# A two-layer encoder on one core: the second layer's attention stage with every engine's instructions in program order

## The chip, the cores and the metric

The kernel runs on one core of a Trainium2 chip. The core has five engines with queues of their own: TensorE (PE; its weight loads are listed as PEld), VectorE (DVE), ScalarE (ACT), GpSimd (POOL) and SyncE (SP), from which nearly all DMA transfers are issued. The metric is the device time of one execution in microseconds. For the kernel before it is 1228.63 us, the median of three runs (1226.69 to 1229.92).

## The reference

The reference is a trunk of two pre-norm attention layers on 1024 tokens of width 1024, in float32, with a final RMSNorm. Only the second layer matters here:

```
def odd_layer(x, mem_n, table, norm_g, w_in, ...):
    h = rmsnorm(x, norm_g)
    q1, q2, k1, k2, v, xq, gate = _split(h @ w_in, ODD_SPLITS)
    ...
    # 6 heads, in blocks of 128 queries:
    s = einsum("ibqhd,ibshd->ibhqs", qi, kk) * (D ** -0.5)
    p = softmax(s + rel_bias, axis=-1)
    w = p[0] - lam * p[1]
    y_c = einsum("bhqs,bshe->bqhe", w, v)
    ...
    y_c = rmsnorm(y_c, subln_g) * (1.0 - lam_init)
    y_x = memory_cross_attention(xq, mem_n, w_mem_kv)    # 4 heads, 256 memory tokens
    y = concatenate([y_c, y_x]) * silu(gate)
    return x + y @ w_out
```

Each of the six heads has two score maps; their softmaxes are subtracted with a factor lam, and the result weighs v.

## The kernel before

The kernel is written with a framework in which the program text issues instructions on named engines and takes tiles from pools with a tag and a number of buffers. At compile time the framework simulates the engines with a model of durations, and draws up each engine's queue from it: of the instructions that are ready, the one that the text has first. So an instruction that waits in the model can be passed by a later one of the same engine, and a load can move far ahead of its place in the text. On the chip each queue then runs as drawn up. `tc.issue_after(ins)` adds an order to single instructions; the text uses it in a few places (L1511 to L1515, and where finish() is called).

The second layer's attention is one call of run_steps over 56 steps: 8 cross-attention steps of 128 queries, then 6 heads with 8 blocks of 128 queries. Iteration i of its loop traces, in this order:

1. hooks(i). For i above 9 this is early.step(), up to 32 times, so for i = 10 to 41. It stores the piece of the output weight that the iteration before made (two DMAs, wo10h/wo10l or wo11h/wo11l), loads the next piece (wor, 128 KB), copies it on ACT (L270) and subtracts on POOL (L271): a split into a high and a low part. For i = 3 it loads the first bias tile.
2. hop of step i - 1: a DMA that copies the finished weights e into er, the form in which they are transposed.
3. s1 of step i: TensorE makes the two score maps (sc, eight matmuls, L1505 and L1514) into both PSUM buffers with the tag S; for each map DVE adds the bias and takes the minimum (L1520) and ACT exponentiates (L1523). In the second block of a head the next head's bias tile is loaded (toep, with two copies on POOL). At a head's first block the projections of its k and q are finished ahead of s1.
4. Two pulls of the projection jobs, eight matmuls each (acc, L329). A job is one 128-column tile of the layer's input projection, 48 matmuls in two halves of 512 tokens, so with three pulls an iteration each half takes an iteration. Where a job starts, the next job's weights are loaded (wr, two DMAs of 256 KB), cast on DVE (wh, L241) and subtracted on POOL (wl, L243). At the end of a half its consumer is traced: for k a cast on ACT (L1419), a subtraction on DVE (L1420) and four row DMAs (ck); for q a cast on ACT (L350), a subtraction on DVE (L351) and four row DMAs (cq), high and low parts in turn; for v a copy on ACT and four transposes (tv) later on; for a gate two instructions. The jobs of a head come as v, gate, then the next head's k and q.
5. Posts, one of each pair in turn. d1, in odd iterations: TensorE's ssqc, two activations on ACT (L1567) and a power on POOL (L231). d2, in even ones: TensorE's rbcc, DVE's L1578 and POOL's product with the gate (L1581); with a head's last pair the store of y.
6. s3, in even iterations, for the pair that ended with step i - 3: 16 matmuls (oc), ACT's copy (L1550), DVE's add (L1551), ACT's square (L1553), DVE's L1556.
7. s2 of step i - 2: eight transposes in two halves of four (te, L580), each half with a cast on ACT (L347) and a subtraction on DVE (L348) into PT.
8. finish of step i: DVE's L1528, L1530 and L1532 make the weighted difference of the two maps in e.
9. One pull of eight matmuls, or none more when the projections are over: then the pulls, two an iteration, run the first part of the output projection (pre, L702), for which y is loaded back in chunks (yr).

Buffers that bear on the order: the tag wr has two buffers, shared by wor, the job weights and the chunks of y; the PSUM tag T has two, shared by ssqc, rbcc, te and tv; the PSUM tag S has two, both taken by one step.

Of the kernel before, what the change touches and what calls it, by code (L numbers as in the profile page):

```python
# [3 lines left out]

# [1 line left out]

# [82 lines left out]
class Jobs:  # L89
# [59 lines left out]
    def drain(self):  # L149
        self.step = 10 ** 9  # L150
        while self._advance():
            pass


@with_exitstack
def encoder_kernel(ctx, tc, A):
# [76 lines left out]
    def load_w(src, after=None, fast=False):  # L233
        his, los = [], []
        for kh in range(2):
            raw = wp.tile([P, 4, P], F32, tag="wr", name="wr", bufs=2)
            dma(raw, src[:, 4 * kh:4 * kh + 4, :])
            hi = wp.tile([P, 4, P], F32R, tag="wh", name="wh", bufs=4)
            lo = wp.tile([P, 4, P], F32R, tag="wl", name="wl", bufs=4)
            with (tc.issue_after(after[0]) if after else nullcontext()):  # L240
                nc.vector.tensor_copy(hi, raw)  # L241
            with (tc.issue_after(after[1]) if after else nullcontext()):
                (nc.vector if fast else nc.gpsimd).tensor_tensor(out=lo, in0=raw, in1=hi, op=ALU.subtract)  # L243
            his.append(hi)
            los.append(lo)
        return his, los
# [228 lines left out]
    def run_steps(steps, jobs, hooks=None, pace=None):  # L475
        n = len(steps)
        posts = deque()
        p2 = p3 = 0
        finish = None
        for i in range(n + LAG + 1):  # L480
            behind = None
            if jobs is not None:
                jobs.step = i
            if hooks:
                hooks(i)
            if 0 < i <= n and steps[i - 1].hop:
                steps[i - 1].hop()
            if i < n:
                if steps[i].need:
                    jobs.ensure(*steps[i].need)  # L490
                finish = steps[i].s1()
            f = steps[min(i, n - 1)].fill
            if jobs is not None:
                if half[0] and len(wout) >= 8 and jobs.projected():
                    f = pace(i)
                two = f > 1 and p3 < n and p3 + steps[p3].lag + 1 <= i and steps[p3].s3b is not None
                jobs.pull(f - f // 2 - two)
                if hooks:
                    hooks(-1)
            for q in list(posts):  # L500
                q.pop(0)()
                if not q:
                    posts.remove(q)
            if p3 < n and p3 + steps[p3].lag + 1 <= i:
                st, p3 = steps[p3], p3 + 1
                if st.s3 is not None:
                    if st.need3:
                        jobs.ensure(*st.need3)
                    r = st.s3()
                    if r:  # L510
                        posts.append(r)
                    if st.s3b is not None:
                        jobs.pull(two)
                        st.s3b()
            if p2 < n and p2 + steps[p2].lag <= i:
                behind = steps[p2].s2()
                p2 += 1
            if finish:
                with (tc.issue_after(behind.ins) if behind is not None else nullcontext()):
                    finish()  # L520
                finish = None
            if jobs is not None:
                jobs.pull(f // 2)
                if hooks:
                    hooks(-1)
        while posts:
            for q in list(posts):
                q.pop(0)()
                if not q:
                    posts.remove(q)  # L530
# [276 lines left out]
    last = [None]  # L807
# [185 lines left out]
    jobs = Jobs(jl, ld)  # L993
# [73 lines left out]
    steps = x_steps(M, X, gates, 3, lambda h, qb: (Xq[h], qb * P), 0)  # L1067
# [393 lines left out]
    jobs = Jobs(jl, lambda j: load_w(j["src"], fast=j["tag"] in FAST or j["tag"] == "g7"))  # L1461
# [16 lines left out]
    steps = x_steps(M, X, gates, 3, lambda h, qb: (Xq1[(h, qb // 4)], (qb % 4) * P), 1)  # L1478
# [115 lines left out]
        if i < 0:  # L1594
            wout_hook(1, jobs, "g5", r2)

    run_steps(steps, jobs, hooks1, lambda i: 2)
    jobs.drain()
    left.close()
    st1 = ExitStack()  # L1600
    out_proj(1, None, st1)
# [72 lines left out]
```

## Time and profile before

| | |
|---|---|
| median of 3 runs | 1228.63 us (1226.69 to 1229.92) |
| the profiled execution's span | 1228.9 us |
| TensorE busy | 1196.5 us (97%) |
| DVE busy | 801.1 us (65%) |
| ACT busy | 663.1 us (54%) |
| POOL busy | 436.3 us (36%) |
| the stage of the change | about 628 to 1161 us of the span |
| mean granted TensorE clock | 0.996 |

The profile is of one execution. A row of a timeline has the start and the duration of an instruction (or of a run of like ones, x their number), its engine, its line, its operation, the tiles it writes and reads, and in brackets how long the engine was idle ahead of it and what ended that. "SPq" rows are DMA issues on SyncE; L175 is the helper through which all of them go. The rows of DMA issues grouped by tile end with the KB of each and the median time from issue to landing. Busy TensorE is modelled and overlaps from one matmul to the next: the spacing of their starts says more than their durations.

### The profile page before, as it was taken

The page shows a single profiled execution, that of the slowest core. Times are in us where ns is not written, and L with a number is a line of the kernel's source. Part 1 is how long each engine was busy: PE and PEld are TensorE (multiplying, and loading weights), DVE is VectorE, ACT ScalarE, POOL GpSimd, SP SyncE. Part 2 cuts the span into 40 slices and gives each one's busy share as a digit, 9 for nine tenths or more (in the row PEclk, how much of TensorE's full clock was granted, in tenths as well). Part 3 has the DMA queues.
Part 4 walks back from the last instruction along what each step waited for, and adds up shares of the span by engine and source line. Part 5 has one row for each costly group of instructions (what it writes and reads, how often), then busy time and mean ns, then how long its engine had stood idle before and what let it go on. Part 6 is the DMA issues. An engine that isn't in the chain of part 4 may idle for free.

```text
span 1228.9 us, 19560 instructions
## 1 busy us (share of the span) xinstructions
PE 1196.5 (97%) x6614; PEld 988.4 (80%) x6614; DVE 801.1 (65%) x1495; ACT 663.1 (54%) x1477; POOL 436.3 (36%) x414
## 2 busy tenths in 40 slices
PE   6999999999999999999999999999999999999997
PEld 5788888888888777888888777777787777777886
DVE  5547665377778878635365866766767767667544
ACT  6248754366667766636157744555545454445332
POOL 5023365366665455437112222333143231301100
PEclk9999999999999999999999999999999999999999
DMA  6664445545465565457645445355363452468354
GB/s 257 200 194 147 163 172 163 166 160 207 163 233 209 208 227 191 151 196 237 186 158 156 153 146 164 121 183 163 124 187 125 153 171 105 149 212 285 121 192 155
DMA packets 114304, 216.70 MB, mean 176 GB/s; under 512 B 13302, under 2 KB 47478, under 8 KB 114204
## 3 DMA queue, kind: packets, MB, share of 16 engines
q1 hardware_dynamic: 114060, 215.25, 52.5%
q8 instruction: 53, 0.87, 0.3%
q14 instruction: 47, 0.39, 0.1%
q10 hardware_dynamic: 144, 0.20, 0.0%
HBM read 87.71 MB, written 39.86 MB: 104 GB/s over the span
## 4 chain that ended last, share of the span: by engine, by line
PE 47%; DVE 2%; DMA 1%; issue 1%; ACT 1%; POOL 0%; POOLq 0%; SPq 0%; DVEq 0%; ACTq 0%
PE acc L329 24%; PE po L702 5%; PE oc L1545 3%; PE sc L1505 3%; PE te L580 3%; PE sc L1514 2%; PE pre L702 2%; PE oc L1547 2%; DMA wr<-in_w_in 1%; PE ssqc L1563 1%; PE ox L656 0%; PE rbcc L1576 0%; PE tv L439 0%; PE sx L543 0%; DVE e L1520 0%
## 5 line engine op out<-in xcount | busy, mean ns | idle before, releaser
L329 PE MATMUL acc<-h,wh 128*128 128x512 f32 x1536 | 499.5, 398 | 1.6 <-DVE h L351 0.8
L329 PEld LDWEIGHTS acc<-h,wh 128*128 128x128 f32 x1536 | 282.4, 188 | 65.7 <-issue 7.9
L329 PE MATMUL acc<-h,wl 128*128 128x512 f32 x768 | 303.8, 396 | 1.5 <-POOL wl L243 1.2
L243 POOL TENSOR_TENSOR wl<-wr,wh 128x512 fp32r<-128x512 f32 x94 | 124.8, 1329 | 286.3 <-DVE wh L241 155.0
L1523 ACT ACTIVATE e<-e,mn 128x1024 f32<-128x1024 f32 x96 | 110.0, 1148 | 117.0 <-DVE mn L1520 116.9
L329 PEld LDWEIGHTS acc<-h,wl 128*128 128x128 f32 x768 | 144.3, 188 | 34.9 <-issue 4.4
L1114 POOL TENSOR_TENSOR e<-e,rz 128x1024 f32<-128x1024 f32 x48 | 91.6, 1910 | 84.2 <-DVE rz L1113 57.8
L1520 DVE CUSTOM_DVE_ANT_0 e<-sc,toep 128x1024 f32<-128x1024 f32 x96 | 113.5, 1218 | 8.0 <-PE sc L1514 7.3
L580 PEld LDWEIGHTS te<-identr,er 128*128 128x128 f32 x896 | 92.2, 143 | 18.8 <-PE sa L543 2.2
L580 PE MATMUL te<-identr,er 128*128 128x128 f32 x896 | 99.9, 246 | 4.3 <-DVE O L1578 1.4
L348 DVE TENSOR_TENSOR PT<-te,PT 128x512 fp32r<-128x512 f32 x112 | 74.3, 687 | 42.8 <-ACT PT L347 39.2
L241 DVE CAST wh<-wr 128x512 fp32r<-128x512 f32 x112 | 58.2, 522 | 42.9 <-PE acc L329 17.3
L348 DVE TENSOR_TENSOR PTl<-te,PTh 128x512 fp32r<-128x512 f32 x112 | 74.0, 684 | 9.4 <-ACT PTh L347 8.9
L1545 PE MATMUL oc<-PT,v 128*128 128x512 f32 x192 | 69.8, 403 | 0.7 <-DVE ckl L1420 0.7
L1532 DVE SCALAR_TENSOR_TENSOR e<-e,mr 128x1024 f32<-128x1024 f32 x48 | 66.3, 1381 | 1.5
L347 ACT CAST PT<-te 128x512 fp32r<-128x512 f32 x112 | 62.7, 589 | 7.2 <-PE te L580 6.7
L347 ACT CAST PTh<-te 128x512 fp32r<-128x512 f32 x112 | 62.2, 586 | 7.9 <-PE te L580 7.1
L702 PE MATMUL po<-woh,yh 128*128 128x512 f32 (+1 forms) x172 | 65.7, 382 | 0.0
L702 PE MATMUL po<-woh,yl 128*128 128x512 f32 (+1 forms) x172 | 65.5, 381 | 0.0
L702 PE MATMUL po<-wol,yh 128*128 128x512 f32 (+1 forms) x172 | 65.3, 380 | 0.0
L1105 DVE TENSOR_REDUCE mn<-sb 128x1 f32<-128x1024 f32 x48 | 58.3, 1216 | 7.0 <-PE sb L543 6.6
L350 ACT ACTIVATE yh<-yr 128x256 fp32r<-128x256 f32 (+2 forms) x56 | 24.0, 447 | 66.2 <-DMA yr<-ysc 37.5
(211 smaller groups left out, 2358.7 us busy)
## 6 DMA issues: line engine op xcount, KB each, us to landing
er<-e SPq DMA_DIRECT2D x112, 512.0 KB, 3.0
wr<-in_w_in SPq DMA_DIRECT2D x96, 256.0 KB, 3.0
ysc<-gy SPq DMA_DIRECT2D x16, 512.0 KB, 2.7
cq<-sg SPq DMA_DIRECT2D x64, 128.0 KB, 2.5
ck<-sg SPq DMA_DIRECT2D x48, 128.0 KB, 2.3
er<-e SPq DMA_DIRECT2D x12, 384.5 KB, 2.6
xpsc<-xh SPq DMA_DIRECT2D x18, 256.0 KB, 2.6
xr<-xpsc SPq DMA_DIRECT2D x9, 512.0 KB, 3.6
```

The source lines that it names most:

```text
L243: (nc.vector if fast else nc.gpsimd).tensor_tensor(out=lo, in0=raw, in1=hi, op=ALU.subtract)
L329: lastmm[0] = nc.tensor.matmul(acc, a, b[:, k, c0:c0 + n], start=(i == 0), stop=(i == 23))
L347: nc.scalar.copy(hi, src)
L348: return nc.vector.tensor_tensor(out=lo, in0=src, in1=hi, op=ALU.subtract)
L580: nc.tensor.transpose(to[:, i * P:(i + 1) * P], e[0][:, k * P:(k + 1) * P], idt)
L702: lastmm[0] = nc.tensor.matmul(acc, a, b, start=(start and n == 0), stop=(stop and n == 2))
L1105: nc.vector.tensor_reduce(out=mn, in_=Sp, op=ALU.min, axis=AX.X)
L1114: nc.gpsimd.tensor_tensor(out=et, in0=et, in1=rz.to_broadcast([P, 1024]), op=ALU.mult)
L1520: nc.vector.tensor_tensor_reduce(out=et, in0=Sp, in1=toeps[h][:, w0:w0 + 1024], scale=1.0, scalar=BIG, op0=ALU.add, op1=ALU.min, accum_out ...
L1523: nc.scalar.activation(et, et, AF.Exp, bias=mn[:, m:m + 1], scale=-1.0, accum_out=z[:, m:m + 1])
L1532: nc.vector.scalar_tensor_tensor(out=es[0], in0=es[1], scalar=c, in1=es[0], op0=ALU.mult, op1=ALU.add)
L1545: nc.tensor.matmul(acc, V[:, kt, 0, :], ph.both[:, kt, :], start=(kt == 0), stop=(kt == 7), skip_group_check=True)
```

## The change

The stage's call of run_steps and the drain behind it are wrapped in a context that runs over all instructions traced inside it, in the order of the text. For each of the five engines, SyncE with its DMA issues included, it adds an edge from each instruction to the one that the text has before it on that engine. The edges order the queues at compile time and add no wait on a semaphore. Instructions ahead of the stage and behind it get no edge.

```
+@contextmanager
+def in_order(tc, engines):
+    bb = tc.nc.cur_bb.bb
+    seen = bb.instructions[-1]
+    yield
+    traced = bb.instructions
+    start = next(k for k in reversed(range(len(traced))) if traced[k] is seen) + 1
+    last = {}
+    for i in traced[start:]:
+        if i.engine not in engines:
+            continue
+        if i.engine in last:
+            tc.add_manual_dep(i, last[i.engine].name,
+                              mybir.DependencyInfo(mybir.DependencyClass.NoSync, mybir.DependencyReason.DATA),
+                              reason="in_order")
+        last[i.engine] = i
...
-    run_steps(steps, jobs, hooks1, lambda i: 2)
-    jobs.drain()
+    with in_order(tc, (mybir.EngineType.PE, mybir.EngineType.Activation, mybir.EngineType.Pool, mybir.EngineType.DVE, mybir.EngineType.SP,)):
+        run_steps(steps, jobs, hooks1, lambda i: 2)
+        jobs.drain()
```

More of the change, by code (lines that the diff above doesn't have):

```diff
@@ L2 @@
 from collections import deque
-from contextlib import ExitStack, nullcontext
+from contextlib import ExitStack, contextmanager, nullcontext
 import numpy as np
```

## The prediction, made before the result was known

> **What bounds the kernel now.** I read the page first, then busy time by stretch, then the engines' timelines over one pair of iterations near 802 us.
>
> ```profile
> span 1228.9 us, 19560 instructions
> PE 1196.5 (97%) x6614; PEld 988.4 (80%) x6614; DVE 801.1 (65%) x1495; ACT 663.1 (54%) x1477; POOL 436.3 (36%) x414
> ```
>
> The profiled span, 1228.9 us, lies 0.02% from the median 1228.63, so the sum is made on the span and carried over unchanged. TensorE is the bound; every microsecond in which it waits is added to the end. By stretch, over the stage that the change wraps (columns: PE, PEld, DVE, ACT, POOL busy):
>
> ```profile
> core 0: us, PE busy (x) PEld busy (x) DVE busy (x) ACT busy (x) POOL busy (x), PEclk, DMA share, GB/s
> 628.00:696.00 68.00, 67.54 (x395) 56.17 (x394) 43.00 (x79) 51.55 (x137) 16.76 (x16) 1.00 0.45 146
> 696.00:1012.00 316.00, 313.68 (x1647) 247.73 (x1646) 220.94 (x399) 160.13 (x327) 98.61 (x103) 1.00 0.49 158
> 1012.00:1082.00 70.00, 70.00 (x369) 55.82 (x369) 48.02 (x88) 32.82 (x64) 14.94 (x13) 1.00 0.34 112
> 1082.00:1161.00 79.00, 78.99 (x426) 62.21 (x425) 55.75 (x104) 38.41 (x84) 8.01 (x11) 1.00 0.67 228
> sum 533.00, PE 530.21 PEld 421.93 DVE 367.71 ACT 282.90 POOL 138.31; mean PE 132.55 PEld 105.48 DVE 91.93 ACT 70.73 POOL 34.58
> ```
>
> TensorE is idle for 533.00 - 530.21 = 2.8 us of the whole stage. That is the most that another order can win there; it can lose far more.
>
> **The order now, against the text.** An odd iteration (one whose post is d1) and the even one behind it, on TensorE:
>
> ```profile
> 802.18 1.07 PE L1505 MATMUL sc<-ck,cq 128*128 128x512 f32 x4
> 807.62 0.50 PE L1563 MATMUL ssqc<-ones,sqc 128*128 128x2 f32 x4
> 807.98 0.52 PE L580 MATMUL te<-identr,er 128*128 128x128 f32 x4
> 808.34 0.46 PE L329 MATMUL acc<-h,wh 128*128 128x512 f32 x1
> 808.87 0.45 PE L580 MATMUL te<-identr,er 128*128 128x128 f32 x4
> 810.62 1.07 PE L1505 MATMUL sc<-ck,cq 128*128 128x512 f32 x4
> 816.05 0.38 PE L1576 MATMUL rbcc<-ident,rz 128*128 128x128 f32 x2
> 819.05 0.81 PE L580 MATMUL te<-identr,er 128*128 128x128 f32 x8
> 821.62 1.07 PE L1505 MATMUL sc<-ck,cq 128*128 128x512 f32 x4
> ```
>
> This is nearly the text's order already (scores, 16 projection matmuls, post, eight transposes, 8 projections). One departure: at 808.34 two projection matmuls stand between the two halves of te. There are two PSUM slots with the tag T; ssqc holds one until ACT's L1567 has read it, so the second half of te waits for L1567. Call that half te2. TensorE's order alone costs little; the other queues feed it. ACT, POOL and SP in the same iteration, and the landing times of the two loads over 696 to 1012 us:
>
> ```profile
> 802.38 0.59 ACT L1419 CAST sg<-acc 128x512 fp32r<-128x512 f32 x1 [0.83 <-PE acc L329]
> 802.87 0.41 ACT L270 CAST wos<-wor 128x256 fp32r<-128x256 f32 x1
> 805.49 1.16 ACT L1523 ACTIVATE e<-e,mn 128x1024 f32<-128x1024 f32 x1 [2.22 <-DVE mn L1520]
> 807.69 0.18 ACT L1523 ACTIVATION_READ_ACCUMULATOR e<-e,mn 128x1 f32 x1
> 808.15 0.41 ACT L1567 ACTIVATE z<-ssqc,es 128x1 f32<-128x1 f32 x2 [0.28 <-PE ssqc L1563]
> 803.35 0.96 POOL L271 TENSOR_TENSOR wos<-wor,wos 128x256 fp32r<-128x256 f32 x1 [5.02 <-ACT wos L270]
> 789.12 4.28 SPq L175 DMA_DIRECT2D wor<-in_w_out  x2
> 803.00 2.41 SPq L175 DMA_DIRECT2D ck<-sg  x4
> 805.51 0.53 SPq L175 DMA_DIRECT2D er<-e  x1
> 806.14 0.53 SPq L175 DMA_DIRECT2D wo10h<-wos  x1
> 806.77 0.68 SPq L175 DMA_DIRECT2D wo10l<-wos  x1
> 807.50 0.45 SPq L175 DMA_DIRECT2D wr<-in_w_in  x1
> wr<-in_w_in SPq DMA_DIRECT2D x34, 256.0 KB, 3.2
> wor<-in_w_out SPq DMA_DIRECT2D x30, 128.0 KB, 2.3
> ```
>
> The piece of output weight that L270 casts at 802.87 was loaded in the stretch from 789.12: SP issues wor a good iteration ahead. In the text it is not ahead. Early.step, in hooks(i) ahead of everything else of iteration i, issues the two stores of the piece before, then the load of wor, and behind that stand, in the same breath, ACT's cast (L270) and POOL's subtraction (L271). The scores' exponentials (L1523) come after L270 on ACT.
>
> **The change, part by part.** It adds no work. It gives SP this order at an iteration's start: the four row DMAs of the projection half that has just ended (only k and q jobs have them), two stores, wor, the er hop, then, where a job starts, the next job's two wr loads.
>
> *Odd iteration behind a k half.* Count from the start of the scores (802.18 in the rows). The row DMAs begin 0.82 later and free SP at 805.51, 3.33 after. Two stores take 0.63 + 0.73 by the spacing 806.14, 806.77, 807.50: wor is issued at 4.69 and lands 2.3 later, at 6.99. L270, 0.41: 7.40. Two exponentials, 805.49 to 807.87: 2.38, so 9.78. L1567, 0.41: 10.2. TensorE could start te2 at 808.34, which is 6.16. It waits 4.1 us, and nothing may run in between, since the 8 projections stand behind te2. The er hop behind wor is not late, since er is read an iteration on, past the next scores and 16 projections; POOL's bias copies for the next head stand behind L271 and are used six iterations on; the gates' products and stores of y feed only the stage's end. These cost nothing as long as SP and POOL have their present idle time.
>
> *Even iteration behind a k half.* Here a job starts, and two wr loads with DVE's casts (L241) stand ahead of d2's L1578, which frees the T slot of rbcc for te2:
>
> ```profile
> 815.11 0.42 DVE L241 CAST wh<-wr 128x512 fp32r<-128x512 f32 x1
> 816.47 0.48 DVE L1578 SCALAR_TENSOR_TENSOR O<-O,misc,rbcc 128x256 f32<-128x256 f32 x1 [0.93 <-PE rbcc L1576]
> 821.87 1.29 DVE L1532 SCALAR_TENSOR_TENSOR e<-e,mr 128x1024 f32<-128x1024 f32 x1
> 823.07 0.68 DVE L351 SCALAR_TENSOR_TENSOR sg<-acc,sg 128x512 fp32r<-128x512 f32 x1
> ```
>
> wor, wr0 and wr1 need three buffers of a tag that has two, so wr1 waits until L271 has released wor: landing 6.99, L270 0.41, L271 0.96, wr1 issued at about 8.45, landed 3.2 later at 11.65, cast 0.42, L1578 0.48, hence te2 at 12.55. Now te2 could start at 819.05 + 0.36 (one half takes 807.98 to 808.34), which is 8.79 behind the scores at 810.62. The wait is 3.8 us.
>
> *Behind q halves.* q's rows alternate high and low; the low part is DVE's L351, behind L1532. In the odd case L1532 is itself late, since the even iteration's DVE was held (rows end about 1.4 later: 5.5 us); in the even case some 0.65: 4.4 us. Per head 4.1 + 3.8 + 5.5 + 4.4 = 17.8 us. Early.step runs for i = 10 to 41, four k and q pairs: 71 us.
>
> Bounds of one such wait: above, a landing 0.9 later (wr's 3.2 instead of wor's 2.3); below, the two stores at er's 0.53 each, 0.3 less. With 16 waits: 66 to 85 us. I take 71, made of rows of the very iteration.
>
> *v and g halves* have no row DMAs; SP reaches wor early and ACT is not held. What is left is te2's wait for L1567: 808.56 against 808.34, some 0.3 us in 16 odd iterations, and v's transposes (tv) needing a T slot that te still holds, about 1.1 us a head, six heads. In the text ACT's square (L1553), which waits for DVE's add, stands ahead of the casts of te, which is in that 1.1. Together 12 us; bounds 4 and 20.
>
> *The end of the stage.* Without projections an iteration pulls 8 matmuls, not 16, ahead of ssqc:
>
> ```profile
> 1122.71 0.52 PE L580 MATMUL te<-identr,er 128*128 128x128 f32 x4
> 1125.22 0.45 PE L580 MATMUL te<-identr,er 128*128 128x128 f32 x4
> ```
>
> Nine matmuls fill 1123.07 (1122.71 + 0.36) to 1125.22. In order, that is a wait of 2.15 us, three times: 6.5. The y chunks (three, ACT casting behind a fresh load) I put at 1.5 each: 4.5. Together 11, bounds 4 and 20. The cross-attention steps (i up to 9) have SP nearly free and no early load: 2, bounds -3 and 8.
>
> Sum: 71 + 12 + 11 + 2 = 96 us. With 1228.63 that is 1325. Bounds of the terms together: 66 + 4 + 4 - 3 = 71 to 85 + 20 + 20 + 8 = 133, so 1300 to 1362 if the mechanism is right.
>
> The wr landing is a place where a page speaks for less. The Trainium skill, "DMA: Bandwidth & Descriptors", section "Anatomy of one DMA", has for transfers that GpSimd issues about 2.0 us fixed plus bytes over 436 GB/s; 256 KB would then land in an estimated 2.6 us where this trace has 3.2. With it the even waits shrink by 0.6 each, eight times, and the result would be 1320; the trace's 3.2 decides.
>
> **The rivals.**
> *No slower.* If wor lands before ACT wants it, nothing in the chain is late. The place is SP's queue at an iteration's start; the point is an issue by 0.6 us behind the scores' start (L270 must end by 805.49, so 3.31 - 0.41 - 2.3), against my 4.69. Then the stage's 2.8 us of idle could even go: 1225.8 to 1229. For it: TensorE's order is the text's almost throughout. Against it: four row DMAs of 2.41 us stand ahead. That the edges bind nothing gives 1228.6, the same side.
>
> *Only the PSUM waits.* The loads hide, te2 and the end of the stage cost: 12 + 11 + 2, so 1253. For it: in 808.34 to 808.87 the present order pays for just this wait. Against it: the same row DMAs.
>
> *Every early iteration waits.* If v and g halves too bring SP late (through the shared buffers of wor and wr), 32 x 4.1 + 25 = 156: 1385. Against it: no DMA hangs on the end of those halves.
>
> *The clock falls.* TensorE does nothing after 1222.5; the clock (the figure ahead of the DMA share) behind that:
>
> ```profile
> 1222.50:1224.00 1.50, 0.00 (x0) 0.00 (x0) 0.93 (x3) 0.51 (x2) 0.28 (x1) 1.00 0.00 0
> 1224.00:1225.50 1.50, 0.00 (x0) 0.00 (x0) 0.55 (x1) 0.61 (x1) 0.27 (x1) 0.98 0.02 5
> 1225.50:1227.00 1.50, 0.00 (x0) 0.00 (x0) 0.00 (x0) 0.00 (x0) 0.00 (x0) 0.50 0.86 330
> ```
>
> After some 3 us of idling TensorE is granted half speed. My sixteen waits are 3.8 to 5.5 us. If each brought that on and the clock came back only after as long again, it would cost 3 x 0.5 = 1.5 us each, 24 in all: 1349. No gap of such length in the stage shows it now. The Trainium skill says as much in "TensorE: Matmul & The Clock Gate", section "What's actually happening": half rate after an idle window of about 3.4 us, and the window runs freely, so that a wait of 4 us need not cover one. The trace's fall agrees; no run here shows the return.
>
> **How the numbers follow.** The forecast, 0.60; every early iteration, 0.12; the clock, 0.10; only the PSUM waits, 0.10; no slower, 0.08 with the edges that bind nothing. A measurement here can tell 0.3%, 3.7 us. The no-slower case reaches 1225.8 at best, inside that, but a gain elsewhere isn't excluded: faster 0.02, same 0.06, slower 0.92. The predicted time is 1325. The range, 8 in 10: below, half of the sixteen waits and none of the small terms, 1229 + 35 = 1264, leaves out the PSUM case and no change; above, 1385 takes in the clock and most of the every-iteration case.
>
> **What would show it.** Right: SP's waits name fewer POOL releases ahead of wor; ACT's L270 waits for DMA wor by 2 to 5 us in k and q iterations and not in v and g; TensorE's waits list te behind ACT z (odd) and behind DVE O L1578 (even), some 8 times each at 4 us; DVE's L241 waits for wr. The heads without early.step (1012 to 1082 now) keep their length within 4 us. Wrong: te hardly waits and the stage is as long as before; or the wait sits at sc or acc, meaning another queue holds TensorE; or the granted clock drops below 0.98 in the stage.

## The result, and the profile after

The changed kernel takes 1382.0 us, the median of four runs (1379.84 to 1389.26); the kernel before, run beside it, takes 1227.95 (1226.69 to 1229.92). The ratio is 1.1265, with a 95% interval of 1.1235 to 1.1294: slower by 154 us where 96 were forecast. The value lies inside the predicted range, 3 us below its upper end. In the profile of after every line number is 18 higher than in that of before.

The page of after, its totals and its row of the granted TensorE clock:

```profile
span 1379.8 us, 19520 instructions
PE 1245.6 (90%) x6614; PEld 1020.1 (74%) x6614; DVE 810.3 (59%) x1495; ACT 660.9 (48%) x1477; POOL 433.1 (31%) x414
PEclk9999999999999999999889999899889899999899
```

The instructions of the engines are as many as before, engine by engine. TensorE is idle for 1379.8 - 1245.6 = 134.2 us, where it was idle for 1228.9 - 1196.5 = 32.4: 102 us more. The other 49 us of the span's growth are in its busy time: the same 6614 matmuls took longer, and the clock's row, with a 9 in every slice before, now has eights in the stage (mean over the span 0.954 against 0.996). Busy time that grows with the same work, beside a lower granted clock, points at the clock; what it cost is taken up further down.

By stretch, cut where a head's first scores start (up to head 1; heads 1 to 3; head 4; the rest; columns as in the prediction's first table):

```profile
686.50:794.90 108.40, 87.29 (x412) 67.31 (x412) 61.41 (x105) 46.21 (x99) 21.69 (x23) 0.87 0.37 121
794.90:1105.20 310.30, 262.48 (x1249) 205.02 (x1248) 170.98 (x301) 119.16 (x247) 73.92 (x78) 0.91 0.37 117
1105.20:1194.40 89.20, 81.95 (x418) 64.30 (x418) 54.06 (x100) 37.93 (x76) 19.48 (x20) 0.96 0.36 115
1194.40:1379.80 185.40, 161.46 (x783) 129.23 (x781) 93.54 (x174) 61.84 (x137) 16.43 (x23) 0.93 0.51 171
```

TensorE waits the largest share of its time, and its clock is lowest (0.87), up to head 1, behind the crossing from cross-attention; next come heads 1 to 3, where Early.step and the loads of k and q weights run (0.91). It waits least in head 4, which has Early.step for two iterations only. The row of before for heads 1 to 3:

```profile
753.22:990.96 237.74, 236.32 (x1250) 187.26 (x1249) 165.90 (x299) 120.91 (x246) 72.54 (x77) 1.00 0.48 153
```

Of the 72.6 us by which these three heads grew, 46.4 are idle time and 26.2 are longer busy time with the same matmuls. What TensorE waited for, over the whole span (us in total, times, longest):

```profile
PE te L598 <- DVE O L1596: 30.4, 12, 5.5
PE te L598 <- ACT z L1585: 30.4, 19, 5.0
...
PE po L720 <- ACT yh L368: 8.1, 1, 8.1
...
PE ox L674 <- DVE PT L366: 4.7, 1, 4.7
PE sc L1523 <- ACT e L650: 4.6, 1, 4.6
```

The first two are the waits of te2 that the prediction named, behind d2 and behind d1. The last three are single ones at the two ends of the stage. One step back, what ACT and DVE waited for in the stage (628 to 1310 us):

```profile
ACT wos L288 <- DMA wor<-in_w_out: 93.2, 17, 7.5
...
DVE wh L259 <- DMA wr<-in_w_in: 98.1, 45, 8.0
...
SPq L193 <- POOL wl L261: 26.5, 11, 7.3
```

The last row has a like one before, where SP, far ahead in its queue, stood for POOL to release a buffer of wr; such waits of SP in the stage fell from 93 to 27 us, since SP now comes late to the loads:

```profile
SPq L175 <- POOL wl L243: 93.2, 39, 4.3
```

Now the same pair of iterations as in the prediction, here around 852 us. TensorE:

```profile
852.02 1.07 PE L1523 MATMUL sc<-ck,cq 128*128 128x512 f32 x4
...
857.81 0.51 PE L598 MATMUL te<-identr,er 128*128 128x128 f32 x4
862.09 0.75 PE L598 MATMUL te<-identr,er 128*128 128x128 f32 x4 [3.77 <-ACT z L1585]
...
866.17 1.65 PE L1523 MATMUL sc<-ck,cq 128*128 128x512 f32 x4
...
875.19 0.46 PE L598 MATMUL te<-identr,er 128*128 128x128 f32 x4
878.04 0.75 PE L598 MATMUL te<-identr,er 128*128 128x128 f32 x4 [2.39 <-DVE O L1596]
```

And SP, ACT and DVE, whose rows explain the two waits:

```profile
852.83 2.40 SPq L193 DMA_DIRECT2D ck<-sg  x4
855.27 0.58 SPq L193 DMA_DIRECT2D wo10h<-wos  x1
855.90 0.45 SPq L193 DMA_DIRECT2D wo10l<-wos  x1
856.45 0.40 SPq L193 DMA_DIRECT2D wor<-in_w_out  x1
...
871.67 3.16 SPq L193 DMA_DIRECT2D wr<-in_w_in  x2
...
852.22 0.59 ACT L1437 CAST sg<-acc 128x512 fp32r<-128x512 f32 x1 [0.24 <-PE acc L347]
859.06 0.40 ACT L288 CAST wos<-wor 128x256 fp32r<-128x256 f32 x1 [6.25 <-DMA wor<-in_w_out]
859.37 1.14 ACT L1541 ACTIVATE e<-e,mn 128x1024 f32<-128x1024 f32 x1
861.64 0.39 ACT L1585 ACTIVATE z<-ssqc,es 128x1 f32<-128x1 f32 x2
...
875.50 0.43 DVE L259 CAST wh<-wr 128x512 fp32r<-128x512 f32 x1 [4.60 <-DMA wr<-in_w_in]
877.01 0.59 DVE L259 CAST wh<-wr 128x512 fp32r<-128x512 f32 x1 [1.09 <-DMA wr<-in_w_in]
877.52 0.47 DVE L1596 SCALAR_TENSOR_TENSOR O<-O,misc,rbcc 128x256 f32<-128x256 f32 x1
```

The odd iteration is read from the left: SP's four row DMAs, two stores, and only then wor; ACT, with nothing to do from 852.8 on, stands 6.25 us before the cast L288, because the exponentials that it could run are queued behind it; L1585 ends at 862.0, and te2 starts at 862.09. That is 10.07 us behind the scores' start, where the prediction had 10.2. In the even iteration DVE stands before the casts of wr with L1596 behind them, and te2 starts 11.87 behind the scores (the prediction had 12.55).

The durations show one thing more: te2 takes 0.75 us where the half ahead of it takes 0.46 to 0.51, and the next scores take 1.65, not 1.07. The granted clock (the figure behind POOL's) around the odd wait, around the even one, and in a like even iteration of the next head, where a wait of 2.70 us ends at 981.04:

```profile
857.13:860.54 3.41, 1.18 (x11) 0.96 (x9) 0.20 (x2) 1.48 (x4) 0.73 (x1) 1.00 0.62 220
860.54:863.95 3.41, 1.86 (x7) 1.67 (x8) 1.15 (x2) 2.55 (x7) 0.69 (x1) 0.50 0.02 5
...
867.37:870.78 3.41, 3.41 (x16) 2.27 (x15) 2.62 (x4) 0.00 (x0) 0.00 (x0) 1.00 0.68 157
874.20:877.61 3.41, 1.45 (x11) 1.19 (x10) 1.02 (x3) 1.99 (x5) 1.54 (x2) 1.00 0.46 142
...
976.60:980.01 3.41, 1.75 (x13) 1.44 (x11) 0.43 (x1) 2.28 (x5) 1.51 (x2) 1.00 0.52 172
...
981.04 0.54 PE L598 MATMUL te<-identr,er 128*128 128x128 f32 x4 [2.70 <-DVE O L1596]
```

The clock falls within the odd wait, at 860.54, and is full again at 867.37, so that TensorE runs at half speed for 5 us behind a wait of 3.77. In the even iteration it is at half from 877.61 to 881.02; behind the wait that ends at 981.04 it stays full. The last section says what tells these cases apart.

### The profile page after: what moved, and what is told of

The parts are those of the page before. It is cut to its first block, busy times and chain, and to the rows that moved or that the text cites. A ratio compares the mean times of both kernels' runs of the same rounds, so it can differ in the third digit from the quotient of the medians.

```text
span 1379.8 us, 19520 instructions
## 1 busy us (share of the span) xinstructions
PE 1245.6 (90%) x6614; PEld 1020.1 (74%) x6614; DVE 810.3 (59%) x1495; ACT 660.9 (48%) x1477; POOL 433.1 (31%) x414
## 4 chain that ended last, share of the span: by engine, by line
PE 28%; DMA 7%; ACT 7%; DVE 7%; issue 4%; SPq 4%; POOL 0%; ACTq 0%; POOLq 0%; DVEq 0%
PE acc L347 14%; PE po L720 4%; SPq L193 4%; DMA wr<-in_w_in 4%; DMA wor<-in_w_out 2%; ACT e L1541 2%; PE oc L1563 2%; PE pre L720 2%; DVE PT L366 2%; PE sc L1523 2%; PE te L598 1%; DVE e L1538 1%; PE sc L1532 1%; PE oc L1565 1%; DMA yr<-ysc 1%
## 5 line engine op out<-in xcount | busy, mean ns | idle before, releaser
L347 PE MATMUL acc<-h,wh 128*128 128x512 f32 x1536 | 514.8, 410 | 4.8 <-ACT vraw L452 3.4
L347 PEld LDWEIGHTS acc<-h,wh 128*128 128x128 f32 x1536 | 294.8, 195 | 75.5 <-issue 11.7
L347 PE MATMUL acc<-h,wl 128*128 128x512 f32 x768 | 312.5, 407 | 1.2 <-POOL wl L261 1.2
L261 POOL TENSOR_TENSOR wl<-wr,wh 128x512 fp32r<-128x512 f32 x94 | 122.5, 1307 | 283.4 <-DVE wh L259 191.0
L347 PEld LDWEIGHTS acc<-h,wl 128*128 128x128 f32 x768 | 149.6, 195 | 35.8 <-issue 4.4
L598 PE MATMUL te<-identr,er 128*128 128x128 f32 x896 | 106.8, 254 | 72.1 <-DVE O L1596 30.4
L259 DVE CAST wh<-wr 128x512 fp32r<-128x512 f32 x112 | 68.4, 614 | 125.4 <-DMA wr<-in_w_in 103.8
L289 POOL TENSOR_TENSOR wos<-wor,wos 128x256 fp32r<-128x256 f32 x32 | 27.7, 866 | 183.5 <-ACT wos L288 183.5
L1523 PE MATMUL sc<-ck,cq 128*128 128x512 f32 x192 | 58.6, 427 | 7.1 <-ACT e L650 4.6
L1550 DVE SCALAR_TENSOR_TENSOR e<-e,mr 128x1024 f32<-128x1024 f32 x48 | 62.1, 1294 | 1.7
```

Source lines behind the costliest of these rows:

```text
L347: lastmm[0] = nc.tensor.matmul(acc, a, b[:, k, c0:c0 + n], start=(i == 0), stop=(i == 23))
L598: nc.tensor.transpose(to[:, i * P:(i + 1) * P], e[0][:, k * P:(k + 1) * P], idt)
L1523: full = nc.tensor.matmul(Sps[m][:, c], C[h][(m, qb // 4)][:, qc], C[h]["k"][m][:, c], start=True, stop=False)
```

## The experiments

My theory: the loss is made by loads that stand right ahead of their casts in the text, wor ahead of ACT's exponentials (odd iterations) and wr ahead of DVE's L1596 (even ones), with smaller costs from the order of the computing engines. Rivals: that order alone, whatever the loads do; and TensorE's clock as a cost of its own. Each kernel is the changed one with the edit shown, was run once, and stands against a run of the kernel before on the same chip (1224.4 to 1228.1 us).

All times at a glance, with the lengths of the parts, worked out from the starts of each head's first scores in TensorE's timeline (us; the parts add up to the profiled span, up to 2 us under the time; those of before are from the profile ahead of the prediction):

| kernel | time | up to head 1 | heads 1 to 3 | head 4 | rest of the span |
|---|---|---|---|---|---|
| before | 1227.95 | 753.2 | 237.7 | 78.7 | 159.3 |
| after | 1382.0 | 794.9 | 310.3 | 89.1 | 185.4 |
| free_early | 1345.5 | 793.0 | 276.9 | 87.7 | 186.2 |
| free_loads | 1338.2 | 781.6 | 286.5 | 83.9 | 184.4 |
| free_both | 1298.3 | 779.1 | 251.1 | 82.6 | 183.7 |
| prefetch | 1377.7 | 794.0 | 298.7 | 99.9 | 183.3 |
| prefetch2 | 1350.0 | 797.1 | 278.2 | 88.4 | 184.5 |
| prefetch_late | 1301.4 | 776.4 | 256.1 | 84.7 | 182.5 |
| all_but_sp | 1293.3 | 776.6 | 255.8 | 84.1 | 175.0 |
| sp_only | 1237.9 | 752.9 | 243.1 | 78.7 | 161.4 |
| pe_only | 1255.8 | 769.2 | 242.1 | 80.7 | 162.0 |
| sp_act | 1274.8 | 758.4 | 261.1 | 87.6 | 165.9 |
| warm | 1381.0 | 798.9 | 305.3 | 90.1 | 184.9 |
| warm2 | 1371.8 | 800.3 | 294.5 | 89.6 | 185.5 |

**Taking the loads out of the order.** The edges skip what Early.step traces (free_early), what the jobs' loader traces, DMAs and casts (free_loads), or both (free_both); those instructions go where the framework's planner puts them. The edits, shortened:

```
+        with free(tc):          # notes the names traced inside
             early.step()
...
+    def free_load(j):
+        with free(tc):
+            return load_w(j["src"], fast=...)
...
-        if i.engine not in engines:
+        if i.engine not in engines or i.name in FREED:
```

> All five queues in program order, but the instructions of early.step (two stores, the load of wor, L270's cast, L271's subtraction) carry no edge. Theory of the prediction (row DMAs, stores, wor, L270, exponentials, L1567 in one chain, and wr1 waiting for wor's buffer): the odd waits of the four heads go and the even ones shrink to under 1 us, with the half-speed matmuls behind them: 8 x (4 + 2) + 8 x (3 + 2) = about 88 us off 1382, so 1285 to 1305. Rival, that TensorE's, VectorE's and ScalarE's own order costs most and the loads little: over 1340.

> All five queues in program order, but the instructions of the job weights' loads (two DMAs wr, the cast to wh, the subtraction to wl) carry no edge. Theory of the prediction: the even waits behind VectorE's L1578 go (8 x 5 = 40 us with the slow matmuls), and so does most of the 16 us that the cross-attention steps lost; the odd waits stay: 1320 to 1340. Rival, that the order of the compute engines costs most: over 1365.

> Both groups, early.step and the job weights' loads, carry no edge; all else is in program order. Theory of the prediction: what is left is the waits for PSUM buffers, the end of the stage and their slow matmuls: 1255 to 1280. Rival (order of the compute engines): over 1320.

free_loads fell where it was expected. free_both is 18 us above its range, and free_early, at 1345.5, lies where its rival had it (over 1340): the computing engines' order costs more than I thought, and what is left with both groups freed is the most that the rival can claim. TensorE's waits in free_early:

```profile
PE te L611 <- DVE O L1609: 23.0, 10, 4.2
PE te L611 <- ACT z L1598: 16.1, 17, 2.4
```

The waits behind ACT z halved and the longest fell from 5.0 to 2.4: the odd ones were wor's. Of those behind DVE O three quarters stayed, though Early.step no longer stood ahead of wr in SP's queue. So one step of my prediction is in doubt, that the even wait comes from wr1 waiting for the buffer that wor holds; prefetch2 below, where wor has a buffer of its own, settles it. Both groups freed take 84 us away (36 and 44 one by one), and 73 us against the kernel before remain.

**Which engines' order.** The tuple of engines is the only edit, for instance (engine names shortened):

```
-    with in_order(tc, (PE, Activation, Pool, DVE, SP)):
+    with in_order(tc, (PE, Activation, Pool, DVE)):
```

> TensorE, ScalarE, VectorE and GpSimd in program order, SyncE's queue left to the framework's order. Theory of the prediction: the loads move ahead again and ScalarE and VectorE find them landed, so only PSUM waits and the end of the stage are left: 1250 to 1275. Rival, that the compute engines' order costs by itself: over 1330.

> Only SyncE's queue in program order. Theory of the prediction: the loads are as late as with all five, but the compile-time model sees that and puts other instructions of TensorE, ScalarE and VectorE ahead of the waiting ones, so little is lost: 1232 to 1262. Rival, that late loads cost by themselves: over 1320.

> Only TensorE's queue in program order. Theory of the prediction: the waits for the PSUM tag T alone (12 us over the heads, 6.5 at the end), loads early: 1238 to 1256. Rival, that TensorE's order carries the loss: over 1320.

> Only SyncE's and ScalarE's queues in program order. Theory of the prediction: ScalarE waits at L270 for wor as with all five (some 4 us in k and q iterations), so te's second half is as late, but TensorE may put projections in between: 1240 to 1290. If the loss is all of the chain whatever TensorE does: over 1320.

Without SP in the order, 89 us of the loss go; with SP alone in it, the kernel loses 13.5 (against its own run of before, 1224.4). The order of SP is thus dear together with a computing engine that cannot step past the late load: with ACT also in order, 50 us are lost. That total was expected, its place was not: te's waits behind ACT z are 3.3 us there, and TensorE's largest wait in the stage is that of the next projection for a PSUM buffer that ACT has yet to copy out (L452), since ACT stands before wor:

```profile
PE acc L347 <- ACT vraw L452: 14.8, 3, 5.5
```

all_but_sp lost 68, more than expected, but far less than its rival had (over 1330). Its largest wait in the heads:

```profile
PE te L598 <- ACT z L1585: 19.9, 22, 3.3
```

It is te2's wait for the PSUM slot of ssqc, with no late load in it: twenty-two times some 0.9 us. pe_only shows where the rest of that starts. It came out at 1255.8, at the upper end of its range, but not by the waits that were expected. Its rows at the crossing from cross-attention to head 0, and the stretch of its first four blocks of head 0 beside that of the kernel before:

```profile
673.22 0.70 PE L1523 MATMUL sc<-ck,cq 128*128 128x512 f32 x2
677.00 1.22 PE L1523 MATMUL sc<-ck,cq 128*128 128x512 f32 x2 [3.07 <-ACT e L650]
...
673.22:720.21 46.99, 36.79 (x170) 27.78 (x170) 31.90 (x56) 24.42 (x53) 9.81 (x11) 0.82 0.33 116
...
673.32:704.53 31.21, 30.50 (x170) 22.66 (x170) 25.77 (x49) 22.33 (x49) 9.76 (x10) 1.00 0.41 143
```

The second score map needs the PSUM buffer that the last cross-attention step's exponential (L650) has yet to read, and in the text's order TensorE has nothing to run ahead of it. pe_only reaches head 0 when the kernel before does (673.22 against 673.32) and head 1 16 us later; the three heads behind that cost 1.5 us more each. The 16 us arise in those four blocks: 9.5 of them are idle time, and 6.3 are the same 170 matmuls taking longer, at a mean clock of 0.82.

**The load one iteration earlier, in the text.** Here all five engines stay in order, and the text is what is edited. prefetch issues wor one iteration ahead, into a tag of its own with two buffers; for the room, O and sq get one buffer. prefetch_late also traces a job's casts (wh, wl) at the third pull behind the job's start, which is in the next iteration. prefetch2 gives O its second buffer back and loads wor into a single buffer in finish(), at the end of the iteration ahead. The edits, shortened:

```
prefetch:
-                raw = wp.tile([P, 512], F32, tag="wr", name="wor", bufs=2)[:, 0:256]
-                dma(raw, w_out...)
+                for m in (self.n - 1, self.n):      # this piece and the next
+                    if m < 32 and m not in self.ahead:
+                        t = self.ahead[m] = wp.tile([P, 256], F32, tag="we", name="wor", bufs=2)
+                        dma(t, w_out...)
+                raw = self.ahead.pop(self.n - 1)
...
+                    O = M.pl.tile([P, 256], F32, tag="O", name="O", bufs=1)
prefetch_late, besides:
+            dma(raw, src[:, 4 * kh:4 * kh + 4, :])
+            late_on[0].later.append(lambda raw=raw: cast(raw))
prefetch2, in place of prefetch's edits:
                 def finish():
+                    early.fetch()      # wor of the next piece, tag "we", bufs=1
```

> All five engines stay in the text's order, but the text itself loads the piece of output weight (wor) one iteration earlier than it is cast, into buffers of its own (O and sq give up their second buffer for the room). My theory: ACT's cast finds wor landed, so the odd iterations' waits of about 5 us at te go as they did with early.step free of order, while the even ones, which wait for the landing of wr and DVE's casts behind it, stay: 1335 to 1355, and TensorE's te behind ACT z falls from 30 to under 12 us in the waits. Rival, that the lateness comes from the engines' order and not from where the load stands: 1370 to 1390.

> As the one above, and the text also casts a job's weights (wh, wl) at the job's third pull, not right behind their two DMAs, so that DVE does not wait for a landing ahead of L1578. All engines in the text's order. My theory: both kinds of waits go, and what is left is that of the kernel with both groups free of order: 1285 to 1315, with te behind DVE O under 6 us in the waits. Rival, that even waits come from DVE's order and not from the landing: above 1335.

> The earlier load of wor once more, without the fault of the first such kernel, in which O had one buffer only and ACT's copy of oc waited for POOL's gating (63 us of waits on ACT). Here the text loads wor at the end of the iteration ahead of its cast, into one buffer of its own; O keeps two, sq one. All five engines in the text's order. My theory: odd waits of about 5 us in k and q iterations go (te behind ACT z from 30 to at most 18 us, the longest under 2.5), even ones stay (te behind DVE O 20 to 33 us): 1335 to 1358. Rival, that where the load stands makes no difference: 1370 to 1390.

prefetch missed: 1377.7. In ACT's waits stands the reason, one that I had built in myself:

```profile
ACT O L1575 <- POOL gy L1606: 63.3, 9, 11.2
```

With one buffer for O, ACT's copy of oc waits until POOL has gated the pair before, which in even iterations is late. prefetch2, without that, came in at 1350.0, as expected. Its waits of TensorE, and behind them the timeline of DVE and POOL in an even iteration:

```profile
PE te L607 <- DVE O L1606: 29.5, 11, 4.8
PE te L607 <- ACT z L1595: 9.1, 15, 2.4
```

```profile
870.07 0.43 DVE L259 CAST wh<-wr 128x512 fp32r<-128x512 f32 x1 [4.44 <-DMA wr<-in_w_in]
870.63 1.26 POOL L261 TENSOR_TENSOR wl<-wr,wh 128x512 fp32r<-128x512 f32 x1 [7.24 <-DVE wh L259]
870.71 1.46 DVE L259 CAST wh<-wr 128x512 fp32r<-128x512 f32 x1 [0.21 <-DMA wr<-in_w_in]
872.10 0.47 DVE L1606 SCALAR_TENSOR_TENSOR O<-O,misc,rbcc 128x256 f32<-128x256 f32 x1
```

The odd waits went (30.4 to 9.1 us) by moving one load in the text, with every queue still in its order. The even ones stayed: DVE waits for wr's first landing, and L1606 stands behind. The second cast adds to it: it takes 1.46 us, where POOL's subtraction L261 of the first half runs beside it, and 0.43 is what the first one takes. prefetch_late takes just that away, and is at 1301.4; the wait behind DVE O is then 2.0 us in all. Its O has one buffer too, which does not bind when L1606 is on time. The two moves together win 81 us, as much as leaving both groups out of the order (84). That settles it for these two waits: not the order as such, but an order in which a load and its first reader stand together.

**The clock.** Extra work that changes no output: 36 transposes (warm) or 14 matmuls of 512 columns (warm2, shown) into te's PSUM tile, in the 16 iterations of the waits, so that TensorE does not idle.

```
+                if j == 0 and getattr(st, "warm", False):
+                    for i in range(14):
+                        nc.tensor.matmul(T, e[0][:, 0:P], e[0][:, 0:512], start=True, stop=True)
```

> The changed kernel, all five in program order, with 36 more transposes (about 3.2 us) that write the first half of te again in the sixteen iterations where the second half waits long. They add work and take none away; the output is unchanged. If the falling clock is a cost of its own, TensorE keeps it up through the wait and the matmuls behind run at full speed: some 2 us less in each, 1340 to 1355. If the slow matmuls have another cause, the time stays at 1378 to 1390.

> Extra work: 14 matmuls of 512 columns into te's own PSUM tile ahead of te's first half, in the same 16 iterations that had the 36 transposes before; their result is overwritten by te. All in the text's order. If TensorE's lower clock is not on the path (SP, ACT and DVE set when te2 can start, and what the full clock gains behind it is lost ahead of the next one): 1372 to 1388. If the 36 small transposes hid a gain by their own form, so that the clock does cost what the half-speed matmuls show (9.5 us in 12 iterations and some more): 1345 to 1368.

warm did not move (1381.0). warm2 is at 1371.8, 0.2 us under the range for a clock that is not on the path (1372 to 1388) and 4 us above that for one that costs what the slow matmuls show (up to 1368): a single run, 8 us under the fastest of the four of after, which spread over 9.4. The same odd iteration in warm2:

```profile
860.38 3.49 PE L598 MATMUL te<-er 128*128 128x512 f32 x14
...
864.62 0.54 PE L601 MATMUL te<-identr,er 128*128 128x128 f32 x4 [0.46 <-ACT z L1589]
866.90 1.07 PE L1526 MATMUL sc<-ck,cq 128*128 128x512 f32 x4
```

te2 runs at full speed, 10.03 us behind the scores (they start at 854.59), and the next scores follow 2.28 later, not 4.08. Over the twelve iterations of heads 1 to 3 that have these waits (blocks 5, 6, 7 and the next head's first), the time from te2 to the next scores falls from 55.8 to 40.6 us, and that from the scores to te2 rises by 2.6: 12.5 us won, which the total shows as 8 to 10. In warm the first fell by 9.4 and the second rose by 9.6. In three of its twelve iterations one issue on SP took 1.6 to 1.8 us, where it takes 0.4 to 0.5 in after, so that the loads behind it came later; why it did, and what held te2 back in the others, isn't settled. In both, the dummy work itself can be the last to end in even iterations, where te2 starts without a wait behind it, so the 8 to 10 us are what keeping the clock up wins in this way, and the clock's full price may be larger.

## Why the prediction was right, and what it mis-sized

*The mechanism* was right, at its place and nearly to the microsecond. te2 started 10.07 us behind the scores in the odd k iteration (predicted 10.2) and at 11.87 in the even one (12.55). From block 5 of head 1 (counted from 0) to the first block of head 4 TensorE waits at te for 2.4 to 5.0 us in each of the twelve iterations behind k and q halves, and for no more than 1.1 in any other. te's waits behind ACT z and DVE O lead the list, DVE's L259 waits 98 us for wr and ACT's L288 93 us for wor, 6 us at a time in these iterations rather than the 2 to 5 of the forecast. The four v and g iterations from 915.27 take 8.34, 12.31, 8.73 and 10.98 us, against 6.27, 11.92, 8.42 and 11.01 before (from 843.23): 2.7 us together. So the rival in which every early iteration waits landed at the right total, 1385, by the wrong way.

*The total* owes something to luck. The time is 20 us above 1362, where the prediction's own bounds of its terms ended; the range held because its upper end had been moved up for the clock and for the rival in which every early iteration waits. TensorE's idle time grew by 102 us where the terms, all of them waits, came to 96, but the parts differ: these twelve te waits come to 42 us where the sum had 53, and the crossing from cross-attention, put at 2, makes up for it. The other 49 us, longer busy time, were in no term.

*The even wait's cause* was half wrong. The step "wr1 waits until L271 has released wor" does show in after: two issues of wr took 3.16 us. But without it, in prefetch2, DVE's step d2 is held all the same, by wr's own landing behind the row DMAs and stores, and by the second cast beside POOL. There te2 still starts 11.1 us behind the scores: taking that buffer away from wor's path is worth 0.7 us, not the wait. As to the landing, the prediction took 3.2 us from the trace, beside the estimate of 2.6 for transfers issued by GpSimd, worked out from "DMA: Bandwidth & Descriptors", "Anatomy of one DMA", of the Trainium skill; in this iteration the sum with 2.6 (11.95) lay nearer to 11.87, while the profile page of after has a median of 3.4 us for these loads.

*One k, q set* was to cost 17.8 us a head. The four iterations from 852.02 took 14.15, 15.45, 15.46 and 18.19 us, where the kernel before, from 802.18, took 8.44, 11.00, 10.26 and 11.35: 22.2 us. This is not the predicted wait with 4.4 us on top. The prediction had te2 4.1, 3.8, 5.5 and 4.4 us late in the four; against its own starts without a wait (6.16 and 8.79 behind the scores) te2 came 3.9, 3.1, 3.8 and 3.8 late, 14.6 together. The odd q iteration is the one that was over-priced: te2 was due at 11.7 behind the scores and came at 9.96 (11.31 and 9.94 in the next two heads). The other 7.6 us are not in te2's start, and most of them are the clock: from te2 to the next scores the four take 18.7 us, and 12.8 in warm2, which keeps the clock up. The prediction held a clock fall for a rival of 24 us at 0.10; it fell, in eleven of the twelve such iterations of heads 1 to 3 by their time from te2 to the next scores, and behind shorter waits than that rival asked for. It is a further cost on the same waits, and the 49 us of busy time are no measure of it: warm2's busy time, 1275.0 us less 16 x 3.4 for the extra matmuls, is some 1220, so that about half of the 49 is gone there, and 8 to 10 us are won. The prediction also says that no run shows the clock's return. The trace of before does, ahead of the stage: half speed from 419.91 to 423.32 and from 440.39 to 443.80 us, at waits of 1.41 and 2.23, so that falls behind waits shorter than its 3 us were on record.

*The edges of the stage* were the worst terms. By the prediction's terms, the parts should have grown by some 17 us up to head 1, 58 in heads 1 to 3, 6 in head 4 and 13 behind that. They grew by 41.7, 72.6, 10.4 and 26.1. "The cross-attention steps have SP nearly free and no early load: 2" failed. pe_only loses 16 us between head 0 and head 1, at the crossing, and there after has waits of 4.6 (sc behind L650) and 4.7 (ox behind DVE). The reason that I gave spoke of SP only; the wait is for PSUM, on TensorE's own queue, and the clock adds to it. Behind head 4, where the sum had 11 for the end, TensorE is idle for 17 us more than before and busy for 9 more. There is one wait of 8.1 us at po, behind ACT's L368, which waits for a chunk of y, and one of 3.2 at pre behind the same line:

```profile
1320.41 0.61 ACT L368 ACTIVATE yh<-yr 128x128 fp32r<-128x128 f32 x2 [7.83 <-DMA yr<-ysc]
```

It stands in each kernel that has all five engines in order, the three with freed loads included, and not in all_but_sp nor in sp_only, sp_act and pe_only: the chunk's load on SP and the order of the computing engines make it together, and ACT's alone does not (sp_act). My 1.5 us a chunk was a guess without a row.

*The PSUM waits in v and g iterations*, 12 us in the sum, are the one small term that can be tested: in free_both, prefetch_late and all_but_sp, where the late loads are gone, a head still costs 4 to 6 us more than before, where the term gave about 1.7. Those three kernels, made in different ways, agree within 8 us at 68 to 75 us above the kernel before: up to head 1 23 to 26, heads 1 to 3 13 to 18, head 4 4 to 6, the rest 16 to 24. That is the price of the computing engines' order in this text, and my sum had some 25 for it. Which of its waits DVE, ACT and POOL each bring was not taken apart further.

The heads without Early.step were to keep their length within 4 us. Head 4 grew by 10.4, but 9 of it in its first two blocks, which still have Early.step (18.30 and 8.29 us, where the like blocks from 831.88 took 11.35 and 6.27); its other six took 1.5 us more, so that the sign held. "Below 0.98" for the clock in the stage was listed as a sign that the prediction is wrong; at 0.87 to 0.96 it was, in that one point.

## What to carry to other kernels

In a queue in program order, a load and its first reader should stand at least one iteration apart, and the reader should stand behind everything of its engine that is ready earlier: moving one load and one pair of casts in the text won 81 of 154 us with every queue still in order. Price a wait by following the queue of each engine from the start of the iteration, as the odd iteration here, which came out within 0.2 us; but do so for the first and last iterations of a stage too, where the filler work is missing and a PSUM buffer changes owner. A wait can cost more than its length: in heads 1 to 3, 26 of 73 us were matmuls that ran slower. The order of a single queue says little of its price: SP's alone cost 13.5 us, that of all others 68, and both together 154.

## What the runs showed of the hardware

The TensorE clock fell behind shorter waits than expected: the row at 878.04 has te2 at 0.75 us, behind a wait of 2.39 us, where the same four transposes ahead of it took 0.46. The Trainium skill, "TensorE: Matmul & The Clock Gate", section "What's actually happening", gives an idle window of about 3.4 us for the fall to half rate; these runs show it behind waits shorter than that.

What tells the waits apart is where they lie. In the trace of after, the clock changes only at points of a grid of 3.41 us. Of the grid's windows that ran at full clock, all 22 in which TensorE was busy for at most 43% were followed by half speed (1.18 of 3.41 us from 857.13, 1.45 from 874.20), and none with 47% or more was (1.75 from 976.60, though that wait, 2.70 us, is the longer one: the grid cuts it in two). Half speed ended behind windows that were busy for 87% or more, and went on behind those with 75% or less. In the other traces the border of the fall is less sharp: windows with up to 65% were followed by half speed, while others down to 47% were not.

Full speed came back only at 867.37, some 5 us behind the odd wait's end at 862.09. Filling such a wait with matmuls that nobody needs kept the clock up and won 8 to 10 us of 1380, in one run, against 81 for removing the cause of the waits.

DVE's cast of a weight half (L259) took 0.43 us each of the 69 times that POOL was idle in the trace of after, and a median of 0.59, up to 2.00, the 43 times that POOL worked beside it.
